# Order of the opening loads in a two-layer decoder trunk: the first weight tile goes to one queue, a second queue is held back behind an activation

## The chip, the cores and the metric

The kernel runs on one core of a Trainium2 chip. A core has five engines that run side by side, each with its own instruction stream: TensorE (PE, matrix products; its weight loads are a row of their own, PEld), VectorE (DVE), ScalarE (ACT), GpSimd (POOL) and SyncE (SP). Loads from the memory of the chip (DMA) are issued by an instruction of one of these streams; here SP and ScalarE issue the loads of the opening, and each has a queue of its own (SP's is q1 in the profile, ScalarE's is q10). A queue's name followed by q (SPq, ACTq) marks the issuing instruction in the profile.

The metric is device time in microseconds (us), the median of several runs.

## The reference

A decoder trunk of two layers on a sequence of 256 tokens and a model width of 1024, in float32. Every layer is an FFN, a token mixer and a second FFN, with norms around each; the mixer of layer 0 is a gated linear recurrence, that of layer 1 attention. Only the first FFN's beginning matters here:

```
def rms_norm(x, g):
    y = xf * lax.rsqrt(jnp.mean(xf * xf, axis=-1, keepdims=True) + EPS)
    return (y * g.astype(jnp.float32)).astype(x.dtype)

def swiglu(x, w_gate, w_up, w_down):
    return (jax.nn.silu(x @ w_gate) * (x @ w_up)) @ w_down
...
    for layer in range(DEPTH):
        f = swiglu(rms_norm(h, ffn1_pre_g[layer]), ffn1_w_gate[layer], ffn1_w_up[layer], ffn1_w_down[layer])
        h = h + 0.5 * rms_norm(f, ffn1_post_g[layer])
```

`ffn1_w_gate` has 1024 rows and 2816 columns per layer.

## The kernel before

The 256 tokens are two tiles of 128 rows, `h[0]` and `h[1]`, each 1024 columns wide (eight blocks of 128). A weight matrix is read in tiles of 128 x 1024 numbers (`raw`): for the first FFN that is two blocks of 128 rows by 512 columns side by side. Five `raw` buffers go round.

Products are made in a split form for precision: each operand is taken as an upper part, rounded to the product's format (`whi`, `xhi`), and a lower part, the rest (`wlo`, `xlo`). One product is then three: upper by upper, lower weight by upper x, and upper weight by lower x. The upper part of a weight tile is rounded by ScalarE (or by VectorE, where `dve=True`), the lower part is subtracted on VectorE.

x enters the products transposed. `turn(t, a, b, bank)` (L1136) transposes column blocks a to b of token tile t on TensorE; `x_up` (L1142, ScalarE) scales them by the norm's gains and rounds, `x_lo` (L1147, VectorE) makes the lower part. `w_up` and `w_lo` (L1123, L1130) do the same for half a weight tile or a whole one. `products(t, i, order)` (L1153) issues the products of token tile t with weight tile i in a given order: in a code such as `0uu`, `0lu`, `0ul`, the digit is the half of the weight tile, the first letter the weight's part and the second x's part.

The opening, L1101 to L1218, is written out by hand: the order of the lines is the order on each engine. It loads x (`load_h(t, a, b, queue)`, column blocks a to b of tile t) and the first four weight tiles (`load_w(i, a, b, queue)`, halves a to b of tile i), SP's queue being the default. Ahead of it, in program order, stand the load of the gains `grow0` (L113, ScalarE's queue), the set-up of an identity matrix on GpSimd and an activation of one column, `warm` (L119), ahead of which ScalarE loads the table of its functions. `keep_busy(n)` (L121) issues n products of constants that nobody reads. The rest of the program (L1219 on) is laid out by loops and a planner; SP's queue carries all of its weight loads.

Every load announces its end on one of eight semaphores, taken in turn. A load that takes a semaphore a second time waits first until the earlier load on it has landed. So in the opening the ninth load and those after it can wait for earlier ones; in the version before these are: `load_w(1, 1, 2)` on ScalarE's queue waits for `load_h(0, 0, 2)`, `load_w(2, 0, 2)` for the gains, `load_h(1, 4, 8)` for `load_w(0, 0, 1)`, and `load_w(3, 0, 2)` for `load_h(0, 2, 4)`.

The lines of the first products, before:

```
    keep_busy(6)
    gains_T(grow0, 16, 0)
    turn(0, 0, 1, gtbank())
    turn(0, 1, 2, gtbank())
    keep_busy(3)
    x_up(0, 0, 2)
    w_up(0, 0, 1, dve=True)
    x_lo(0, 0, 1)
    w_lo(0, 0, 1)
    w_up(0, 1, 2)
    x_lo(0, 1, 2)
    w_lo(0, 1, 2)
    products(0, 0, "0uu 0ul 1uu 0lu 1ul")
    turn(1, 0, 2, early[0])
```

Of the kernel before, what the change touches and what calls it, by code (L numbers as in the profile page):

```python
# [12 lines left out]
AF = mybir.ActivationFunctionType  # L13
# [31 lines left out]
def trunk_kernel(ctx: ExitStack, tc: tile.TileContext, A: dict, out: bass.AP):  # L45
    nc = tc.nc
# [18 lines left out]
    def gtbank():  # L65
        return psum.tile([P, 512], F32, tag="gt", name=nm("gt"), bufs=2)

    def trbank():
        return psum.tile([P, 512], F32, tag="tr", name=nm("tr"), bufs=2)
# [36 lines left out]
    h = [hpool.tile([P, D], F32, tag=f"h{t}", name=f"h{t}") for t in range(2)]  # L106

    def load_h(t, a, b, q=nc.sync):

        q.dma_start(h[t][:, a * P:b * P], A["x"][0, t * P:(t + 1) * P, a * P:b * P])  # L110
# [5 lines left out]
    mhalf = cpool.tile([P, 1], F32, name="mhalf")  # L116
    nc.gpsimd.memset(mhalf, -0.5)
    warm = cpool.tile([P, 1], F32, name="warm")
    nc.scalar.activation(warm, mhalf, AF.Silu)  # L119

    def keep_busy(n):  # L121

        ps = trbank()
        for _ in range(n):
            nc.tensor.matmul(ps, nc.const_aps.tensor(1.0, (P, P), BF16), nc.const_aps.tensor(1.0, (P, 512), BF16),
                             start=True, stop=True)
# [978 lines left out]
    def load_w(i, a, b, q=nc.sync):  # L1105

        q.dma_start(raws[i][:, a * 512:b * 512].rearrange("p (k n) -> p k n", k=b - a),
                          A["ffn1_w_gate"][0, (2 * i + a) * P:(2 * i + b) * P, :512].rearrange("(k p) n -> p k n", p=P))

    load_h(0, 0, 2)  # L1110
    load_w(0, 0, 1)
    load_w(0, 1, 2, nc.scalar)
    load_h(0, 2, 4)
    load_h(1, 0, 4, nc.scalar)
    load_w(1, 0, 1)
    load_w(1, 1, 2, nc.scalar)
    load_h(0, 4, 8)
# [18 lines left out]
    def turn(t, a, b, bank):  # L1136

        for k in range(a, b):
            tps[t, k] = bank[:, (k - a) * P:(k - a + 1) * P]
            nc.tensor.transpose(tps[t, k], h[t][:, k * P:(k + 1) * P], ident)  # L1140

    def x_up(t, a, b):  # L1142
        for k in range(a, b):
            nc.scalar.activation(xhi[:, k, t * P:(t + 1) * P], tps[t, k], AF.Copy,
                                 scale=gT[:, k:k + 1])
# [19 lines left out]
    gains_T(grow0, 16, 0)  # L1165
    turn(0, 0, 1, gtbank())
    turn(0, 1, 2, gtbank())
    keep_busy(3)
    x_up(0, 0, 2)
    w_up(0, 0, 1, dve=True)  # L1170
    x_lo(0, 0, 1)
# [139 lines left out]
```

## Time and profile before

| what | value |
|---|---|
| median of 3 runs | 1001.75 us |
| the runs | 1003.43, 1001.75, 1001.18 us |
| the profiled execution, its own time | 1001.1 us |
| its span, first to last instruction | 999.4 us |
| its mean granted TensorE clock | 0.998 |
| instructions | 12928 |
| moved by DMA | 178.88 MB, mean 179 GB/s |

The profile is one execution, recorded by the hardware. Its time, 1001.1 us, is 1.7 us more than its span. A row of the timeline reads: start, duration, engine, line of the kernel, operation, what is written, an arrow, what is read, the shapes, how many, and in brackets how long the engine had been idle before and what ended that. A row of the table of stretches reads: from and to, the sum of the window, then for PE, PEld, DVE, ACT and POOL the busy us and the number of instructions, the granted TensorE clock, the share in which the 16 DMA engines were busy, and GB/s. A row on a DMA queue reads: packets, MB, and the time that they took as a share of the 16 engines' time. Busy times of PE include a modelled end of each product, so the distance between two starts is the better measure of its pace.

### The profile page before, as it was taken

How to read it: one execution, taken by the hardware profiler on the slowest of the kernel's cores; microseconds unless marked ns; L12 is line 12 of the kernel's file. 1: busy time of each engine (PE TensorE's matmuls, PEld its weight loads, DVE VectorE, ACT ScalarE, POOL GpSimd, SP SyncE). 2: the span in 40 equal slices, each digit the busy share in tenths (PEclk: the TensorE clock that was granted, in tenths of full speed). 3: DMA queues.
4: the chain of work that ended last, by engine and by line, in shares of the span. 5: the costliest groups of instructions: out<-in, count | busy, mean ns of one | idle time of the engine just before them, and what ended most of it. 6: DMA issues, size and time to landing. Idle time of an engine off the chain costs nothing.

```text
span 999.4 us, 12928 instructions
## 1 busy us (share of the span) xinstructions
PE 991.0 (99%) x4792; PEld 829.4 (83%) x4792; DVE 613.0 (61%) x775; ACT 532.7 (53%) x749; POOL 59.0 (6%) x98
## 2 busy tenths in 40 slices
PE   9999999999999999999999999999999999999997
PEld 6888888899988888888898888888888888888885
DVE  6756554668998555554786655554487576555542
ACT  7545444569986544443564544443466565444431
POOL 2400000100004000000100000000033000000000
PEclk9999999999999999999999999999999999999999
DMA  8867556565336766555467666555455066665531
GB/s 289 308 191 208 183 186 192 158 189 157 119 115 217 216 175 196 182 186 190 130 208 233 172 188 188 189 179 191 157 173 167 15 200 210 190 187 190 190 106 42
DMA packets 92788, 178.88 MB, mean 179 GB/s; under 512 B 11982, under 2 KB 32886, under 8 KB 92726
## 3 DMA queue, kind: packets, MB, share of 16 engines
q1 hardware_dynamic: 91430, 177.16, 55.9%
q8 instruction: 37, 0.61, 0.2%
q10 hardware_dynamic: 464, 0.79, 0.2%
q0 software_dynamic: 832, 0.12, 0.1%
q14 instruction: 25, 0.20, 0.1%
HBM read 176.95 MB, written 1.05 MB: 178 GB/s over the span
## 4 chain that ended last, share of the span: by engine, by line
PE 99%; DMA 0%; DVE 0%; POOLq 0%; ACT 0%; issue 0%; DVEq 0%; SPq 0%; POOL 0%; ACTq 0%
PE mm L185 29%; PE mm L187 29%; PE mm L186 29%; PE tr L499 2%; PE gt L727 2%; PE mm L1159 1%; PE gt L1018 1%; PE mm L192 1%; PE mm L194 1%; PE mm L1045 1%; PE mm L193 1%; PE gt L216 1%; PE tr L1034 1%; DMA raw<-in_ffn_w_gate_dram 0%; PE tr L914 0%; PE tr L796 0%
## 5 line engine op out<-in xcount | busy, mean ns | idle before, releaser
L179 DVE TENSOR_TENSOR wlo<-raw,whi 128x1024 fp32r<-128x1024 f32 (+4 forms) x325 | 391.5, 1210 | 269.6 <-ACT whi L174 267.0
L174 ACT ACTIVATE whi<-raw 128x1024 fp32r<-128x1024 f32 (+4 forms) x325 | 337.8, 1045 | 315.7 <-PE mm L187 252.6
L185 PE MATMUL mm<-whi,xhi 128*128 128x512 f32 (+2 forms) x768 | 304.1, 396 | 0.0
L187 PE MATMUL mm<-whi,xlo 128*128 128x512 f32 (+2 forms) x768 | 298.8, 389 | 0.0
L186 PE MATMUL mm<-wlo,xhi 128*128 128x512 f32 (+2 forms) x768 | 298.1, 388 | 0.0
L187 PEld LDWEIGHTS mm<-whi,xlo 128*128 128x128 f32 x768 | 144.2, 188 | 30.3 <-DVE xlo L251 0.3
L186 PEld LDWEIGHTS mm<-wlo,xhi 128*128 128x128 f32 x768 | 144.5, 188 | 28.0 <-DVE wlo L179 0.3
L185 PEld LDWEIGHTS mm<-whi,xhi 128*128 128x128 f32 x768 | 144.3, 188 | 27.6
L185 PE MATMUL mm<-whi,hhi 128*128 128x512 f32 x352 | 138.6, 394 | 0.0
L187 PE MATMUL mm<-whi,hlo 128*128 128x512 f32 x352 | 137.9, 392 | 0.0
L186 PE MATMUL mm<-wlo,hhi 128*128 128x512 f32 x352 | 137.2, 390 | 0.0
L187 PEld LDWEIGHTS mm<-whi,hlo 128*128 128x128 f32 x352 | 66.1, 188 | 14.4
L186 PEld LDWEIGHTS mm<-wlo,hhi 128*128 128x128 f32 x352 | 66.1, 188 | 14.1
L185 PEld LDWEIGHTS mm<-whi,hhi 128*128 128x128 f32 x352 | 66.1, 188 | 13.5
L200 POOL TENSOR_SCALAR nv<-ss 128x1 f32<-128x1 f32 x24 | 11.6, 484 | 881.6 <-ACT junk L207 881.6
L493 DVE SCALAR_TENSOR_TENSOR prod<-mm,rstd,sil 128x512 f32<-128x512 f32 (+1 forms) x48 | 33.9, 705 | 38.0 <-PE mm L187 34.3
L484 ACT ACTIVATE sil<-mm,rstd 128x512 f32<-128x512 f32 (+1 forms) x48 | 31.2, 652 | 40.2 <-PE mm L187 40.2
L503 ACT ACTIVATE hhi<-tr 128x512 fp32r<-128x512 f32 (+1 forms) x48 | 26.6, 555 | 15.5 <-PE tr L499 15.4
L272 DVE TENSOR_TENSOR t<-mm,gb 128x512 f32<-128x512 f32 x24 | 16.2, 686 | 28.4 <-ACT junk L207 28.4
L504 DVE TENSOR_TENSOR hlo<-tr,hhi 128x512 fp32r<-128x512 f32 (+1 forms) x48 | 30.5, 642 | 1.4
L207 ACT ACTIVATE junk<-mm 128x512 bf16<-128x512 f32 x24 | 14.3, 596 | 31.7 <-PE mm L187 31.7
L185 PE MATMUL mm<-whi,zhi 128*128 128x340 f32 (+2 forms) x80 | 28.3, 354 | 0.0
(196 smaller groups left out, 934.0 us busy)
## 6 DMA issues: line engine op xcount, KB each, us to landing
raw<-in_ffn_w_down_dram SPq DMA_DIRECT2D x88, 512.0 KB
raw<-in_ffn_w_up_dram SPq DMA_DIRECT2D x80, 512.0 KB
raw<-in_ffn_w_gate_dram SPq DMA_DIRECT2D x78, 512.0 KB
raw<-in_rg_w_in_dram SPq DMA_DIRECT2D x20, 504.0 KB
raw<-in_rg_w_out_dram SPq DMA_DIRECT2D x10, 504.0 KB
raw<-in_ffn_w_gate_dram SPq DMA_DIRECT2D x18, 256.0 KB
raw<-in_ffn_w_up_dram SPq DMA_DIRECT2D x16, 256.0 KB
raw<-in_w_kv_dram SPq DMA_DIRECT2D x8, 512.0 KB
```

Source lines behind the costliest of these rows:

```text
L174: up = nc.scalar.activation(hi[:parts, c:c + m], rawv[:, c:c + m], AF.Copy)
L179: low.tensor_tensor(lo[:parts, c:c + m], rawv[:, c:c + m], hi[:parts, c:c + m].bitcast(F32), ALU.subtract)
L185: nc.tensor.matmul(ps, xh, wh, start=first, stop=False)
L186: nc.tensor.matmul(ps, xh, wl, start=False, stop=False)
L187: nc.tensor.matmul(ps, xl, wh, start=False, stop=last)
L272: nc.vector.tensor_tensor(t1[n], pf[n], gb[:, n * 512:(n + 1) * 512], ALU.mult)
L484: nc.scalar.activation(s[:, :nn], ps, AF.Silu, scale=rs[t][:, 0:1])
L493: nc.vector.scalar_tensor_tensor(pr[:, :nn], ps, rs[t][:, 0:1], s, ALU.mult, ALU.mult)
L499: nc.tensor.transpose(tp[:, j * P:(j + 1) * P], pr[:, j * P:(j + 1) * P], ident)
L503: nc.scalar.activation(hv, tp[:, :nn], AF.Copy)
L504: nc.vector.tensor_tensor(lv, tp[:, :nn], hv.bitcast(F32), ALU.subtract)
L727: nc.tensor.matmul(ps[:w, j * S:(j + 1) * S], wv[:, o:o + w], xc[:w, k, :], start=k == 0, stop=k == m - 1)
```

## The change

Three things are changed. The activation of one column on ScalarE writes column 0 of `h[1]`, and no longer the tile `warm` (which stays allocated). As `load_h(1, 0, 4)` writes the same column later, that load, on ScalarE's queue, now waits until the activation has run. The second half of the first weight tile, `load_w(0, 1, 2)`, moves from ScalarE's queue to SP's, behind the first half, and `load_h(1, 0, 4)` comes ahead of `load_h(0, 2, 4)` in program order (they are on different queues). The second `keep_busy` issues two products and not three.

```
     warm = cpool.tile([P, 1], F32, name="warm")
-    nc.scalar.activation(warm, mhalf, AF.Silu)
+
+    nc.scalar.activation(h[1][:, :1], mhalf, AF.Silu)
...
     load_h(0, 0, 2)
     load_w(0, 0, 1)
-    load_w(0, 1, 2, nc.scalar)
+    load_w(0, 1, 2)
+    load_h(1, 0, 4, nc.scalar)
     load_h(0, 2, 4)
-    load_h(1, 0, 4, nc.scalar)
     load_w(1, 0, 1)
     load_w(1, 1, 2, nc.scalar)
...
     turn(0, 1, 2, gtbank())
-    keep_busy(3)
+    keep_busy(2)
     x_up(0, 0, 2)
```

The order of loads on each queue, as built:

| queue | before | after |
|---|---|---|
| SP | `load_h(0,0,2)`, `load_w(0,0,1)`, `load_h(0,2,4)`, `load_w(1,0,1)`, `load_h(0,4,8)`, `load_w(2,0,2)`, `load_h(1,4,8)`, `load_w(3,0,2)` | `load_h(0,0,2)`, `load_w(0,0,1)`, `load_w(0,1,2)`, `load_h(0,2,4)`, `load_w(1,0,1)`, `load_h(0,4,8)`, `load_w(2,0,2)`, `load_h(1,4,8)`, `load_w(3,0,2)` |
| ScalarE | gains, `load_w(0,1,2)`, `load_h(1,0,4)`, `load_w(1,1,2)` | gains, (activation), `load_h(1,0,4)`, `load_w(1,1,2)` |

The waits for a semaphore taken again move with the order: now `load_h(0, 4, 8)` waits for the gains, `load_w(2, 0, 2)` for `load_h(0, 0, 2)`, `load_h(1, 4, 8)` for `load_w(0, 0, 1)`, and `load_w(3, 0, 2)` for `load_w(0, 1, 2)`; `load_w(1, 1, 2)` waits for none. Everything behind the opening stands in the same order on every engine.

More of the change, by code (lines that the diff above doesn't have):

```diff
@@ L118, in trunk_kernel @@
     warm = cpool.tile([P, 1], F32, name="warm")
-    nc.scalar.activation(warm, mhalf, AF.Silu)
+    nc.scalar.activation(h[1][:, :1], mhalf, AF.Silu)
     def keep_busy(n):
@@ L1111, in trunk_kernel @@
     load_w(0, 0, 1)
-    load_w(0, 1, 2, nc.scalar)
+    load_w(0, 1, 2)
+    load_h(1, 0, 4, nc.scalar)
     load_h(0, 2, 4)
-    load_h(1, 0, 4, nc.scalar)
     load_w(1, 0, 1)
@@ L1167, in trunk_kernel @@
     turn(0, 1, 2, gtbank())
-    keep_busy(3)
+    keep_busy(2)
     x_up(0, 0, 2)
```

## The prediction

> **What bounds the kernel now.** I read the page first: its busy shares and its chain of waits followed back from the end.
>
> ```profile
> span 999.4 us, 12928 instructions
> PE 991.0 (99%) x4792; PEld 829.4 (83%) x4792; DVE 613.0 (61%) x775; ACT 532.7 (53%) x749; POOL 59.0 (6%) x98
> PE 99%; DMA 0%; DVE 0%; POOLq 0%; ACT 0%; issue 0%; DVEq 0%; SPq 0%; POOL 0%; ACTq 0%
> ```
>
> TensorE is busy for 991.0 of 999.4 us and the chain that sets the end lies on it for 99%. An edit of the opening can therefore pay only what it takes off the time before TensorE works without a break. The built programs hold the same instructions in the same order on every engine behind the opening, so nothing else moves. Next I read the chain in order of time for the first 14 us.
>
> ```profile
> 1.23 4.38 DMA raw<-in_ffn_w_gate_dram
> ...
> 5.63 0.44 DVE whi L1126
> 6.07 0.14 issue
> 6.20 1.53 PE mm L1159 x5
> ```
>
> The end hangs on the landing of one load, the first half of the first weight tile (call it w0a; w0b is the other half, h0a the first two column blocks of x tile 0, h1a the first four of tile 1, w1a and w1b the halves of the second weight tile). It was issued at 1.23 and had landed 4.38 later, at 5.61; then come its rounding on VectorE, a hand-over of 0.14, and products. So 6.20 us is the figure that the edit can attack. Third, the timeline of that stretch: who issues when, and who waits for what.
>
> ```profile
> 0.80 0.38 SPq L110 DMA_DIRECT2D h<-in_x_dram  x1
> 1.31 0.37 ACTq L1107 DMA_DIRECT2D raw<-in_ffn_w_gate_dram  x1
> 1.71 0.45 ACTq L110 DMA_DIRECT2D h<-in_x_dram  x1
> 2.17 0.43 SPq L1107 DMA_DIRECT2D raw<-in_ffn_w_gate_dram  x1
> 2.53 0.20 ACT L119 ACTIVATE warm<-mhalf 128x1 f32<-128x1 f32 x1
> 2.64 0.43 SPq L110 DMA_DIRECT2D h<-in_x_dram  x1
> 3.12 0.43 SPq L1107 DMA_DIRECT2D raw<-in_ffn_w_gate_dram  x1
> 3.31 0.34 ACTq L1107 DMA_DIRECT2D raw<-in_ffn_w_gate_dram  x1
> 5.82 0.63 ACT L1128 ACTIVATE whi<-raw 128x512 fp32r<-128x512 f32 x1 [0.98 <-DMA raw<-in_ffn_w_gate_dram]
> 6.20 0.47 PE L1159 MATMUL mm<-whi,xhi 128*128 128x512 f32 x1 [0.57 <-DVE whi L1126]
> 6.51 0.39 PE L1159 MATMUL mm<-whi,xlo 128*128 128x512 f32 x1
> 6.74 0.40 PE L1159 MATMUL mm<-whi,xhi 128*128 128x512 f32 x1
> 6.83 0.34 DVE L1149 SCALAR_TENSOR_TENSOR xlo<-gt,gT,xhi 128x128 fp32r<-128x128 f32 x1
> 6.97 0.50 PE L1159 MATMUL mm<-wlo,xhi 128*128 128x512 f32 x1
> 7.32 0.41 PE L1159 MATMUL mm<-whi,xlo 128*128 128x512 f32 x1
> 7.57 0.38 PE L1140 MATMUL mm<-ident,h 128*128 128x128 f32 x2
> ```
>
> ScalarE began w0b's upper part at 5.82, after 0.98 us of waiting for the load: w0b landed only 0.2 behind w0a. Five products run from 6.20, then the transposes of h1a at 7.57. Two gaps exceed the pace of 0.23 (6.51 to 6.74): after 6.20, and 6.97 to 7.32, where the product waited for the `xlo` that VectorE ran from 6.83 to 7.17.
>
> **The loads, part by part.** w0b moves from ScalarE's queue (1.31) to SP's third place; a place in SP's queue is 0.47 (2.17, 2.64), so w0b is issued at 1.70, h0b at 2.17, w1a at 2.64. h1a now waits for the activation (2.53 + 0.20), so it is issued at about 2.8 and not 1.71; behind it on ScalarE's queue only w1b waits (issued about 3.25, before 3.31) and then the first `x_up`, which needs transposes at 3.7 and is not delayed. To see what this does to landings I use bytes: GB/s is KB per ms, so one row of the stretches of 1 us gives KB moved, and the queue rows tell whose.
>
> ```profile
> 1.00:2.00 1.00, 1.00 (x3) 0.30 (x2) 0.00 (x0) 0.76 (x1) 0.32 (x2) 1.00 0.08 25
> 2.00:3.00 1.00, 1.00 (x4) 0.30 (x2) 0.00 (x0) 0.72 (x2) 0.00 (x0) 1.00 0.92 205
> 3.00:4.00 1.00, 1.00 (x5) 0.48 (x4) 0.17 (x1) 0.00 (x0) 0.00 (x0) 1.00 0.89 266
> 4.00:5.00 1.00, 1.00 (x4) 0.42 (x3) 0.00 (x0) 0.62 (x2) 0.00 (x0) 1.00 0.99 329
> 5.00:6.00 1.00, 0.63 (x2) 0.00 (x0) 0.37 (x2) 0.18 (x1) 0.00 (x0) 1.00 1.05 378
> ```
>
> Together 25, 230, 496, 825 and 1203 KB had moved at 2, 3, 4, 5 and 6 us. The next fence has the queue rows, q1 being SP's and q10 ScalarE's: the first two for 0 to 4.5 us, then q10 in 6 to 7, 7 to 8 and 8 to 9.
>
> ```profile
> q1 hardware_dynamic: 305, 0.41, 35.0%
> q10 hardware_dynamic: 156, 0.24, 17.9%
> ...
> q10 hardware_dynamic: 8, 0.01, 5.0%
> ...
> q10 hardware_dynamic: 67, 0.14, 38.1%
> ...
> q10 hardware_dynamic: 71, 0.12, 32.2%
> ```
>
> By shapes h0a is 131 KB, each weight half and h1a 262, the gains row 8. SP's queue had moved h0a and w0a (0.39 MB) at about 4.45, yet w0a landed at 5.61: 1.15 us from nominal last byte to landing. ScalarE's queue had moved 0.27 MB at about 4.65 (0.24 at 4.5) and w0b landed near 5.80: 1.15 again. I use that lag throughout.
>
> *w0a.* With ScalarE's queue silent, 401 KB (gains, h0a, w0a) are through at 3 + (401 - 230)/266 = 3.64, landing at 4.8; at the slower 205 of the stretch before, 3.83 and 5.0. Earlier by 0.6 to 0.8. Rounding 0.44 and hand-over 0.14: the first product could start at 5.4.
>
> *w0b.* It now stands behind w0a in one queue. Nominal end at 663 KB: 4 + (663 - 496)/329 = 4.51, landing 5.66, if h1a stays out. h1a's first bytes are unknown: SP's first load took about 1.05 us from issue to bytes (0.80 to near 1.85, from 25 KB), ScalarE's first weight load about 1.7 (1.31 to near 3.0, as q10 had moved hardly anything by then). From 2.8 that is 3.85 to 4.5. At 4.5 it is too late to matter: 5.66. At 3.85, 456 KB are through, w0b lacks 207, and at half of 329 that takes 1.26: landing 6.26. I take the middle, 4.2: 562 KB through, 101 lacking, 0.61, nominal 4.81, landing 5.96. That is 0.16 *later* than before: w0b no longer has a queue to itself.
>
> [...]
>
> *The products.* ScalarE rounds w0b in 0.63: 5.98 to 6.61, so the third product, the first on w0b, starts at about 6.66 (before 6.74). The two ahead of it, at 5.4 and 5.6, are out of the way. VectorE's first four steps, rounding to the second `xlo`, took 5.63 to 7.17; from 4.82 they end at 6.36, so that `xlo` no longer holds the fifth product. So products at 6.66, 6.89, 7.12, transposes at 7.35 in place of 7.57: **0.22 us earlier**. By the bounds of w0b the third product starts at 6.36 or 6.96 and the transposes at 7.05 or 7.65: 0.52 earlier to 0.08 later.
>
> *h1a* must have landed by 7.35. From 4.2 at half of 329 to 378 (about 180) it needs 1.46, nominal 5.66, landing 6.8: covered, with 0.5 to spare. If first bytes come at 4.5 it lands at 7.1, which only the best case would feel, by 0.05.
>
> *The keep-busy matmul.* Its pace is the distance between the weight loads of the warm-up (rows of the timeline).
>
> ```profile
> 0.83 2.72 PE L125 MATMUL tr<-const-bfloat16-1.0 128*128 128x512 bf16 x6 [0.83 <-PEq L1296]
> 1.21 0.15 PEld L125 LDWEIGHTS <-const-bfloat16-1.0 128*128 128x128 bf16 x1 [0.28 <-issue]
> 1.64 0.15 PEld L125 LDWEIGHTS <-const-bfloat16-1.0 128*128 128x128 bf16 x1 [0.28 <-issue]
> 4.18 1.45 PE L125 MATMUL tr<-const-bfloat16-1.0 128*128 128x512 bf16 x3
> ```
>
> 0.43 each, three from 4.18, so TensorE is free at 5.46 before and at 5.04 after. A product at 5.4 would lose 0.06 to the third; as w0b decides at 6.66, the removal itself is worth 0 here.
>
> **What comes late next.** A gain at 7.35 survives only if the next loads don't hold TensorE.
>
> ```profile
> 9.62 0.63 ACT L1128 ACTIVATE whi<-raw 128x512 fp32r<-128x512 f32 x1 [0.34 <-DMA raw<-in_ffn_w_gate_dram]
> 10.13 0.40 PE L1159 MATMUL mm<-wlo,xhi 128*128 128x512 f32 x1
> 10.37 0.44 PE L1159 MATMUL mm<-whi,xhi 128*128 128x512 f32 x1
> ```
>
> w1b landed at about 9.6 and the product at 10.37 took it without slack (10.13 + 0.23). It was issued at 3.31, 0.2 behind SP's 3.12, yet q10 was idle from 6 to 7 and moved it in 7 to 9: it stood behind what SP had issued. After the change SP's load of 2.64 stands at 3.12 and that of 3.12 at about 3.6, so w1b goes ahead of the latter, straight behind h1a: from 5.66 at about 180, nominal 7.1, landing 8.3; other end unchanged, 9.6. I take it as out of the way.
>
> w1a has 1.32 MB up to and including it: at the last stretch's 378 that is 6 + (1320 - 1203)/378 = 6.31, landing 7.46. VectorE comes free for it when its fifth step ends, 6.61 + 0.68 = 7.3, so it may wait 0.2; TensorE then still has transposes and products of block pair 0 that do not need it.
>
> Sum: 1001.1 (profiled execution: span 999.4 and 1.7 around it) - 0.22 = 1000.9. The median of the runs, 1001.75, lies 0.65 above that execution, so I forecast 1001.5.
>
> **Rivals.** (a) *Swallowed at w1b*: it keeps its landing at 9.6, the product at 10.37 stays, gain 0: 1001.75. For it: no slack there. Against: its new place in the order. (b) *w0a does not land earlier*, because the 1.15 us lag and not sharing sets it: the first product stays at 6.20, the chain is the old one, 1001.75; the 0.6 us by which the bytes come sooner speak against it. (c) *The held-back load collides*: h1a enters at 3.85, w0b lands at 6.26, the transposes are at 7.65: 0.08 lost, 1001.85. (d) *TensorE stays slow*, the slower side. Warm-up matmuls and first products have the same 512 columns, but 0.43 against 0.23 apart: TensorE ran at half pace until somewhere between the third keep-busy (4.18 + 2 x 0.43 = 5.04) and 6.51. The profile's clock column does not show that (1.00 throughout). If the shorter warm-up and the new hole (two products at 5.4 and 5.6, then nothing until 6.66) start the count anew at 5.4, and it takes 4.2 to 5.7 us as it did from 0.83, products go at 0.43 until 9.6 to 11.1: from 6.66 that is 2.9 to 4.4 us, 7 to 10 products, 0.2 each: 1.4 to 2.0 lost less 0.22: 1002.9 to 1003.5. It decides once the hole exceeds what the hole of 5.46 to 6.20 already was (0.74); the new holes are 0.36 and about 0.83. [...]
>
> **How the numbers follow.** Forecast 0.45, (a) 0.17, (b) 0.10, (c) 0.10, (d) 0.15, 0.03 for a larger gain. 0.2% is 2 us, about what a measurement of this kernel can tell from no change; only the top of (d) together with a run like 1003.43 goes past 1003.75: slower 0.05. No case reaches 999.75: faster 0.04. Same 0.91. The likeliest case's own range is 1001.2 to 1001.85; the scatter of the runs and most of (d) widen it to 1000.5 to 1003.1.
>
> **What would show it.** Right: w0a's rounding starts near 4.8, w0b's near 6.0, the third product near 6.66, the transposes of h1a near 7.35 without a wait, w1b's rounding without an idle time before it, and every later product about 0.2 earlier. Wrong: first products 0.43 apart, an idle TensorE ahead of the transposes of h1a, w1b again at 9.6, or w0b's rounding later than 6.3.

## The result, and the profile after

| | before | changed |
|---|---|---|
| median of 16 runs | 1001.40 us | 1002.96 us |
| lowest, highest | 1000.75, 1003.43 | 1001.79, 1005.63 |
| the profiled execution (its span) | 1001.1 (999.4) | 1002.14 (1000.4) |

The changed kernel is slower by 1.6 us: ratio 1.0015, 95% interval 1.0008 to 1.0022. A small gain had been forecast. The first view of the profile after is the chain of waits in order of time, for the first 14 us (start, length, what; line numbers behind L119 are one higher than before).

```profile
2.53 0.21 ACT h L120
2.74 0.02 issue
2.77 5.64 DMA h<-in_x_dram
8.40 0.04 issue
8.45 0.44 PE mm L1141 x2
8.89 0.22 PE tr L1141 x2
```

The chain no longer runs through the first weight half. It runs through the activation, the load that waits for it, x tile 1, issued at 2.77 and landed at 8.40, and the transposes of that tile at 8.45. The timeline shows what stood in front of it.

```profile
2.77 0.36 ACTq L110 DMA_DIRECT2D h<-in_x_dram  x1
4.20 0.43 DVE L1127 CAST whi<-raw 128x512 fp32r<-128x512 f32 x1 [0.22 <-DMA raw<-in_ffn_w_gate_dram]
4.77 0.90 PE L1160 MATMUL mm<-whi,xhi 128*128 128x512 f32 x1
4.93 0.63 ACT L1129 ACTIVATE whi<-raw 128x512 fp32r<-128x512 f32 x1
5.89 0.58 PE L1160 MATMUL mm<-whi,xhi 128*128 128x512 f32 x1
6.30 0.39 PE L1160 MATMUL mm<-wlo,xhi 128*128 128x512 f32 x1
6.53 0.40 PE L1160 MATMUL mm<-whi,xlo 128*128 128x512 f32 x1
8.45 0.44 PE L1141 MATMUL mm<-ident,h 128*128 128x128 f32 x2 [1.52 <-DMA h<-in_x_dram]
10.66 0.63 ACT L1129 ACTIVATE whi<-raw 128x512 fp32r<-128x512 f32 x1 [0.44 <-DMA raw<-in_ffn_w_gate_dram]
```

The first weight tile came far earlier: its halves were being rounded at 4.20 and 4.93 (before 5.63 and 5.82), and the fifth product started at 6.53 (7.32). Then TensorE stood still until 8.45. The transposes, at 7.57 before, are 0.88 later; at the hand-over to the loop-built part, the first product of L185 before and of L186 after, it is 1.04:

```profile
19.26 0.40 PE L185 MATMUL mm<-whi,xhi 128*128 128x512 f32 x1
```

```profile
20.30 0.40 PE L186 MATMUL mm<-whi,xhi 128*128 128x512 f32 x1
```

From there on TensorE loses nothing more: the two spans, 999.4 and 1000.4, differ by 1.0 as well. In the table of stretches the 780 us from 200 to 980 are the same to 0.01 us of TensorE work, the first row from the profile before, the second from after:

```profile
200.00:980.00 780.00, 779.98 (x3846) 658.70 (x3846) 488.18 (x607) 423.70 (x596) 37.53 (x51) 1.00 0.55 173
```

```profile
200.00:980.00 780.00, 779.97 (x3846) 658.70 (x3845) 489.37 (x609) 424.69 (x598) 37.67 (x51) 1.00 0.55 173
```

So the profiled execution lost 1.04 us, all of it ahead of 20 us. The median lost 1.56. The rest shows in the granted clock that each of the 16 runs reports: in nine it is 0.998 or 0.999, their median 1002.24; in seven it is 0.996 or 0.997, their median 1004.18. The first group is 0.84 above before, about what the stall costs. The second has something on top, 1.9 us, that hardly ever met the version before: 2 of its 77 runs beside the experiments had such a clock. (The clock does not sort the runs without fault: one of the nine, with 0.998, took 1003.67.)

The stretches of 1 us of the changed kernel show where x tile 1 was in the meantime (last column GB/s, that is, KB per us).

```profile
1.00:2.00 1.00, 1.00 (x3) 0.30 (x2) 0.00 (x0) 0.76 (x1) 0.32 (x2) 1.00 0.07 23
2.00:3.00 1.00, 1.00 (x4) 0.30 (x2) 0.00 (x0) 0.72 (x2) 0.00 (x0) 1.00 0.86 197
3.00:4.00 1.00, 1.00 (x5) 0.48 (x4) 0.17 (x1) 0.00 (x0) 0.00 (x0) 1.00 1.04 393
4.00:5.00 1.00, 1.00 (x5) 0.53 (x3) 0.80 (x3) 0.69 (x3) 0.00 (x0) 1.00 0.66 175
5.00:6.00 1.00, 1.00 (x4) 0.75 (x4) 1.00 (x3) 0.56 (x1) 0.00 (x0) 1.00 0.65 153
6.00:7.00 1.00, 0.93 (x4) 0.41 (x2) 0.42 (x1) 0.00 (x0) 0.00 (x0) 1.00 0.98 307
```

SP's queue alone moved 393 KB in the stretch from 3 to 4. Then both together fell to 175 and 153, in the two stretches in which ScalarE's queue came in, and in 5 to 6 only 0.07 MB of it were ScalarE's (the first two rows below; q10 is ScalarE's, q1 SP's). In 6 to 7 they were 0.13 (the third row):

```profile
q1 hardware_dynamic: 60, 0.08, 35.2%
q10 hardware_dynamic: 36, 0.07, 29.9%
...
q10 hardware_dynamic: 70, 0.13, 42.5%
```

The same view for 4 to 5 gives ScalarE's queue 0.01 MB, all of it after 4.5. By 5.0 SP's queue had moved 0.77 MB; what it had issued up to 2.17 (`load_h(0, 0, 2)`, both halves of the first weight tile, `load_h(0, 2, 4)`) is 0.79.

### The profile page after: what moved, and what is told of

It is laid out like the page before. It is cut to its first block, busy times and chain, and to the rows that moved or that the text cites. A ratio compares the mean times of both kernels' runs of the same rounds, so it can differ in the third digit from the quotient of the medians.

```text
span 1000.4 us, 12926 instructions
## 1 busy us (share of the span) xinstructions
PE 991.1 (99%) x4791; PEld 829.8 (83%) x4791; DVE 613.4 (61%) x775; ACT 532.6 (53%) x749; POOL 59.2 (6%) x98
## 3 DMA queue, kind: packets, MB, share of 16 engines
HBM read 176.95 MB, written 1.05 MB: 178 GB/s over the span
## 4 chain that ended last, share of the span: by engine, by line
PE 98%; DMA 1%; ACT 0%; DVE 0%; POOLq 0%; ACTq 0%; issue 0%; DVEq 0%; POOL 0%
PE mm L186 29%; PE mm L188 29%; PE mm L187 29%; PE tr L500 2%; PE gt L728 2%; PE gt L1019 1%; PE mm L193 1%; PE mm L195 1%; PE mm L1046 1%; PE mm L194 1%; PE mm L1160 1%; PE gt L217 1%; DMA h<-in_x_dram 1%; PE tr L1035 1%; PE tr L915 0%; PE tr L797 0%
## 5 line engine op out<-in xcount | busy, mean ns | idle before, releaser
L186 PE MATMUL mm<-whi,xhi 128*128 128x512 f32 (+2 forms) x768 | 304.2, 396 | 0.0
L186 PEld LDWEIGHTS mm<-whi,xhi 128*128 128x128 f32 x768 | 144.3, 188 | 27.5
L186 PE MATMUL mm<-whi,hhi 128*128 128x512 f32 x352 | 138.6, 394 | 0.0
L186 PEld LDWEIGHTS mm<-whi,hhi 128*128 128x128 f32 x352 | 66.1, 188 | 13.5
L186 PE MATMUL mm<-whi,zhi 128*128 128x340 f32 (+2 forms) x80 | 28.3, 354 | 0.0
```

The lines of the kernel that those rows point to most:

```text
L186: nc.tensor.matmul(ps, xh, wh, start=first, stop=False)
```

## The experiments

All times are medians; each ratio is against runs of the version before on the same chip (1001.42, 1001.47 and 1001.37 us in the three groups of runs). "Low clock" counts runs whose granted clock was 0.997 or less. An edit is shown against the changed kernel, unless another version is named. Every landing and every start is read from one trace, so differences of a few tenths between two kernels say little. Three theories were open at first: H, the held-back x tile 1 comes too late; Q (later S), starting a second queue beside a busy one slows both; G, the missing warm-up matmul.

**The missing warm-up matmul alone**, against the version before

```
-    keep_busy(3)
+    keep_busy(2)
```

> The version before with one keep-busy matmul less, its only edit. Theory H (the held-back load of x tile 1 comes too late and TensorE waits for it) and rival Q (ScalarE's queue, when it starts beside SP's, slows both for about 1.5 us) expect no change: ratio within 0.9997 to 1.0003, first product at 6.20. Rival G (the shorter warm-up keeps TensorE at half pace for longer) expects a good part of the whole difference of 1.5 us here: 1.0005 to 1.0015, with products 0.43 apart behind 6.20.

Measured: 1001.67 us, ratio 1.0003 (0.9994 to 1.0011). By this interval alone up to 1.1 us could still be here, so it does not settle G. The changed kernel's trace does for its execution: the fifth product stands 0.23 behind the fourth (6.30, 6.53) and TensorE then waits 1.52 us for a load, so a slow start cost it nothing; and none of the four one-queue versions below, with two matmuls as well, is slower than before. The profiled execution here, 1002.55 and the highest of its 11, shows what G meant. The first products were still 0.42 to 0.43 apart, where before they came down to 0.23:

```profile
6.54 0.63 PE L1159 MATMUL mm<-whi,xlo 128*128 128x512 f32 x1
6.97 0.63 PE L1159 MATMUL mm<-whi,xhi 128*128 128x512 f32 x1
7.39 0.63 PE L1159 MATMUL mm<-wlo,xhi 128*128 128x512 f32 x1
```

The full pace came only behind 9.81, and the transposes stood at 8.25 in place of 7.57. The granted clock of this stretch reads 1.00 all the same: the slow pace of the start is seen in the distances and not in that column. Whether it is more frequent with two matmuls is not shown; 4 of 11 runs lay above 1002 us here, and 7 of the 29 of before.

**The change without the hold**

```
-    nc.scalar.activation(h[1][:, :1], mhalf, AF.Silu)
+    nc.scalar.activation(warm, mhalf, AF.Silu)
```

> The change without the hold: the activation writes its own tile, so ScalarE's queue issues the load of x tile 1 at about 1.3 and not 2.8. H: that load lands before 6.8, TensorE does not wait for it, and the time is 0.3 to 0.9 us below the version before (0.9991 to 0.9997). Q: the slow stretch comes at about 3.0 to 4.5 in place of 4.5 to 6.0, the first weight half lands near 5 again and the time is that of before (0.9997 to 1.0003). G: still 0.5 to 1.5 us above before.

Measured: 1002.97 us, 1.0014 (1.0005 to 1.0023), low clock in 6 of 11. H and Q had the time wrong. G had it about right (0.5 to 1.5 us above before), but not the way: the first two products below are 0.31 apart, not 0.43. x tile 1 did come early (TensorE did not wait for it), and now the *second weight half* was late: it stands behind the first in SP's queue, and ScalarE began to round it at 6.91, after 2.07 us of waiting for the load (at 4.93 in the change). On ScalarE's queue x tile 1 and the second half of the second weight tile, which is needed later, had been issued at 1.31 and 1.71.

```profile
6.11 0.47 PE L1160 MATMUL mm<-whi,xhi 128*128 128x512 f32 x1 [1.02 <-DVE whi L1127]
6.42 0.40 PE L1160 MATMUL mm<-whi,xlo 128*128 128x512 f32 x1
7.59 0.50 PE L1160 MATMUL mm<-whi,xhi 128*128 128x512 f32 x1 [0.77 <-ACT whi L1129]
...
8.50 0.63 PE L1141 MATMUL mm<-ident,h 128*128 128x128 f32 x2
```

The third product waited until 7.59 and the transposes came at 8.50, as late as in the change. In the stretches of the same trace DMA moved 381 and 388 in 4 to 6; the slow stretch came in 3 to 4, with 211, at the time that Q had named. The stretches behind 8 show something else, the granted clock (the column ahead of the DMA share):

```profile
8.00:9.00 1.00, 1.00 (x6) 0.77 (x5) 0.60 (x2) 0.00 (x0) 0.00 (x0) 0.62 1.05 391
9.00:10.00 1.00, 1.00 (x6) 0.82 (x5) 0.17 (x1) 0.63 (x2) 0.00 (x0) 0.50 1.05 401
10.00:11.00 1.00, 1.00 (x4) 0.87 (x4) 1.00 (x3) 0.55 (x3) 0.00 (x0) 0.50 1.06 401
11.00:12.00 1.00, 1.00 (x4) 0.79 (x3) 0.93 (x4) 1.00 (x5) 0.00 (x0) 0.68 1.05 393
```

After the holes ahead of 6.11 and 7.59, waits of 1.02 and 0.77 us, TensorE ran at half clock: with the clock at either 1.00 or the 0.50 of the two middle rows, an estimate, it lasted twice what is missing from 1.00 in the four rows, 0.76 + 1 + 1 + 0.64 = 3.4 us. Products were 0.43 apart in it (11.06 and 11.49) and 0.23 behind it (12.27 and 12.50). What sets its length, and how long a wait brings it on, this trace does not show.

**The hold without the move of the weight half**: the version before with only

```
-    nc.scalar.activation(warm, mhalf, AF.Silu)
+    nc.scalar.activation(h[1][:, :1], mhalf, AF.Silu)
```

> The version before with the hold alone: the second weight half stays on ScalarE's queue at 1.31, the load of x tile 1 behind it waits for the activation (2.8). H: that load lands about 1 us later than before and TensorE waits ahead of its transposes: 0.3 to 1 us slower (1.0003 to 1.0010). Q: ScalarE's queue starts near 3.0 as before, the load stands behind the weight half in it anyway, so no change (0.9998 to 1.0003).

Measured: 1003.23 us, 1.0027 (1.0015 to 1.0040), low clock in 3 of 7: the slowest of all. The fifth product is at 6.87, the transposes only at

```profile
9.30 0.44 PE L1140 MATMUL mm<-ident,h 128*128 128x128 f32 x2 [2.00 <-DMA h<-in_x_dram]
```

H had the sign and the place, and about half of the size (1.8 us by the medians; the ratio stands higher, as three of seven runs took 1005 or more). So the hold alone is enough for a loss of this size, and the move without the hold was enough too: in each case one load that TensorE needs next came late.

**All opening loads on SP's queue, nothing held** (the gains stay on ScalarE's):

```
-    nc.scalar.activation(h[1][:, :1], mhalf, AF.Silu)
+    nc.scalar.activation(warm, mhalf, AF.Silu)
...
-    load_h(1, 0, 4, nc.scalar)
+    load_h(1, 0, 4)
...
-    load_w(1, 1, 2, nc.scalar)
+    load_w(1, 1, 2)
```

> All opening loads but the gains on SP's queue, x tile 1 right behind the first weight tile, nothing held, two keep-busy matmuls. H and Q: with ScalarE's queue silent SP's goes on at about 390 KB per us, x tile 1 has landed by 5.5 to 6, the products start at 4.8 and the transposes follow without a wait: 0.5 to 1.2 us below before (0.9988 to 0.9995). If the slow stretch behind 4.5 us has nothing to do with the second queue (the memory or the making of descriptors), it comes here too, x tile 1 lands near 8 and the time is above before.

Measured: 1000.48 us, 0.9990 (0.9981 to 0.9998), from 999.98 to 1000.61, low clock in none of 11. This version beats both kernels, and its runs lie closer together than any other's. H and Q both expected that, so it does not choose between them; G's loss is not here, though it has the two warm-up matmuls as well. x tile 1 was later than forecast (5.5 to 6): TensorE waited 0.34 for it.

```profile
4.68 0.74 PE L1160 MATMUL mm<-whi,xhi 128*128 128x512 f32 x1
...
6.12 0.40 PE L1160 MATMUL mm<-whi,xlo 128*128 128x512 f32 x1
6.86 0.44 PE L1141 MATMUL mm<-ident,h 128*128 128x128 f32 x2 [0.34 <-DMA h<-in_x_dram]
```

**Late issue, or another queue?** The same, but with the hold, so that x tile 1 is issued as late as in the change, only on SP's queue:

```
-    load_h(1, 0, 4, nc.scalar)
+    load_h(1, 0, 4)
...
-    load_w(1, 1, 2, nc.scalar)
+    load_w(1, 1, 2)
```

> The changed kernel with the two loads of ScalarE's queue (x tile 1 and the second half of the second weight tile) at the same places of SP's queue; the hold stays, so SP issues x tile 1 at about 2.8, the same time as the change does on ScalarE's queue. Theory S (what is lost comes from starting a second queue beside a busy one, not from the late issue): x tile 1 lands by 7.5, TensorE waits at most 0.8, time below the version before: 0.9990 to 0.9998. Rival L (the late issue is what costs): it lands near 8.4 as in the change and the time is 1.0008 to 1.0020.

Measured: 1000.92 us, 0.9993 (0.9984 to 1.0002), low clock in none of 11.

```profile
2.76 0.80 SPq L110 DMA_DIRECT2D h<-in_x_dram  x2
...
6.33 0.44 PE L1141 MATMUL mm<-ident,h 128*128 128x128 f32 x2
```

Issued at 2.76, as in the change at 2.77, x tile 1 was there for transposes at 6.33 without a wait, not 8.45. The issue time by itself is not the cause; L falls. But S is not shown by it either, though its numbers came true: DMA slowed here too, on one queue, from 397 KB per us in 3 to 4 to the 226 of the stretch from 4 to 6 (last column), and the edit also changes the order.

```profile
4.00:6.00 2.00, 1.82 (x8) 0.94 (x7) 1.82 (x5) 1.26 (x3) 0.00 (x0) 1.00 0.82 226
```

On SP's queue x tile 1 is issued ahead of all that SP issues later: the hold keeps back `load_h(0, 2, 4)` (here right behind it, the second of the two from 2.76, and at 2.17 in the change) and the second weight tile (3.60, in the change 2.65) too.

**The same place in the order, one queue**: x tile 1 behind the first half of the second weight tile, nothing held (SP's order: `load_w(1, 0, 1)`, `load_h(1, 0, 4)`, `load_w(1, 1, 2)`; the changed kernel's lines otherwise).

```
-    nc.scalar.activation(h[1][:, :1], mhalf, AF.Silu)
+    nc.scalar.activation(warm, mhalf, AF.Silu)
...
-    load_h(1, 0, 4, nc.scalar)
     load_h(0, 2, 4)
     load_w(1, 0, 1)
-    load_w(1, 1, 2, nc.scalar)
+    load_h(1, 0, 4)
+    load_w(1, 1, 2)
```

> All opening loads on SP's queue without the hold, but x tile 1 behind the first half of the second weight tile, which is the order of bytes that the change has by its issue times. S: by then 1.3 MB have to pass at about 320 KB per us, x tile 1 lands at 7 to 7.6, TensorE waits 0.5 to 1.2, ratio 0.9993 to 1.0000. Rival B (the order of bytes explains the loss, the second queue does not): x tile 1 lands near 8.4, ratio 1.0008 to 1.0020.

Measured: 1001.42 us, 1.0000 (0.9991 to 1.0008), low clock in none of 11.

```profile
7.83 0.44 PE L1141 MATMUL mm<-ident,h 128*128 128x128 f32 x2 [1.12 <-DMA h<-in_x_dram]
```

The wait of 1.12 and the ratio are what S expected; x tile 1 landed about 0.2 later than its 7.6. B falls: the order of bytes alone did not make this kernel slower than before. The later place has its price all the same, 0.97 us of the transposes' start and 0.94 of the median against the one-queue version above. What the change loses beyond it, 1.5 us of the median, came only with loads on ScalarE's queue.

**x tile 1 alone on the second queue**, held; the weight half behind it goes to SP:

```
-    load_w(1, 1, 2, nc.scalar)
+    load_w(1, 1, 2)
```

> The changed kernel with only x tile 1 left on ScalarE's queue (held); the second half of the second weight tile goes to SP's queue. S: the start of ScalarE's queue near 4.5 still slows both, x tile 1 lands near 8, TensorE waits over 1 us, ratio 1.0003 to 1.0015. Rival W (the weight half behind x tile 1 on the second queue takes the bandwidth): x tile 1 lands before 7.3 and the ratio is under 1.0000.

Measured: 1001.99 us, 1.0007 (0.9998 to 1.0016), low clock in 4 of 11: those four lie at 1003.3 to 1003.6, the other seven at 1001.5 to 1002.4.

```profile
8.18 0.44 PE L1141 MATMUL mm<-ident,h 128*128 128x128 f32 x2 [1.54 <-DMA h<-in_x_dram]
```

W falls: x tile 1 landed near 8.2 and not before 7.3, and the weight half behind it costs 0.27 (8.45 - 8.18), no more than single traces can differ by. S has its numbers here too (near 8, over 1 us of waiting, 1.0003 to 1.0015), but the interval takes in 1.0000.

**The hole filled**: six keep-busy matmuls put where TensorE stood still.

```
     products(0, 0, "0uu 0ul 1uu 0lu 1ul")
+    keep_busy(6)
     turn(1, 0, 2, early[0])
```

> The changed kernel with six more keep-busy matmuls between the fifth product and the transposes of x tile 1, where TensorE stood still. They take about 1.3 us at full pace and 2.6 at half pace, against a hole of 1.5 to 2. Theory G2 (in many runs the hole also makes TensorE fall back to half pace, which is the spread of 1001.8 to 1005.6): median down to 1002.0 to 1002.5, highest run under 1003.5. Rival (the hole is all there is): median stays at 1002.7 to 1003.2 with the same spread, or rises.

Measured: 1002.24 us, 1.0009 (1.0000 to 1.0018), highest 1003.32, low clock in none of 11. The transposes were at 8.76 in its trace, behind 0.81 of idle time that the six matmuls left, so x tile 1 was as late, yet the seven-in-sixteen share of low clocks is gone, and the median is the 1002.24 that the changed kernel has in its full-clock runs. G2 holds.

**The changed kernel twice more**

> The changed kernel once more, for a second trace. If its loss is one of order, x tile 1 lands between 8 and 9 again and TensorE waits over 1.2 us ahead of its transposes. If the landing of 8.4 was chance, it lands before 7.5. If the clock gate closes behind the hole, the stretches of 1 us show a granted clock of 0.50 for about 3.4 us after 8.

> The changed kernel a third time, with the same expectations as the second.

Measured: 1004.61 us (clock 0.997) and 1002.17 us (0.998), one run each. Transposes at 9.66 after 2.78 of waiting in the first (later than the 8 to 9 expected), at 8.60 after 2.09 in the second; the late landing is no chance. In the first the granted clock fell to 0.50 behind the hole, which is what the expectation calls the closing of the clock gate. The stretches:

```profile
7.00:8.00 1.00, 0.00 (x0) 0.00 (x0) 0.00 (x0) 0.00 (x0) 0.00 (x0) 1.00 1.02 330
8.00:9.00 1.00, 0.00 (x0) 0.00 (x0) 0.00 (x0) 0.00 (x0) 0.00 (x0) 1.00 0.97 342
9.00:10.00 1.00, 0.34 (x2) 0.34 (x3) 0.43 (x1) 0.00 (x0) 0.00 (x0) 0.75 1.02 389
10.00:11.00 1.00, 1.00 (x5) 0.82 (x4) 0.00 (x0) 0.61 (x2) 0.00 (x0) 0.50 1.05 408
11.00:12.00 1.00, 1.00 (x5) 0.90 (x4) 0.95 (x3) 0.34 (x3) 0.00 (x0) 0.50 1.05 361
12.00:13.00 1.00, 1.00 (x4) 0.81 (x3) 0.93 (x4) 1.00 (x5) 0.00 (x0) 0.54 1.03 387
```

TensorE did nothing for two whole stretches, and half clock follows, reckoned as above, for 0.5 + 1 + 1 + 0.9 = 3.4 us. Products were 0.42 and 0.43 apart in it (11.86, 12.28, 12.71), and 0.23 in the second trace, whose clock stayed at 1.00 (10.06, 10.29). At half clock 3.4 us hold the work of an estimated 1.7 at full clock: 1.7 us lost, against the 1.9 between the two groups of the changed kernel's runs.

**x tile 1 in two halves, one queue**, against the one-queue version with nothing held

```
-    load_h(1, 0, 4)
+    load_h(1, 0, 2)
+    load_h(1, 2, 4)
```

> The one-queue kernel with x tile 1 loaded in two halves, so that the first transposes need 131 KB and not 262. If the landing of x tile 1 is what still holds the opening there (0.34 us of idle ahead of its transposes), the first half lands 0.4 to 0.8 earlier, the wait goes and the time falls to 1000.1 to 1000.4 where before runs 1001.4 (0.9986 to 0.9990). If the price of a further load (0.47 of issue, one more semaphore taken twice) eats it: 1000.4 to 1000.8.

Measured: 1000.79 us, 0.9992 (0.9983 to 1.0001). The wait ahead of the transposes went (they start at 6.61), but behind the further load the second weight tile was issued at 3.60 (3.12 without the split), VectorE did not begin to round it before 8.0 (7.84), and TensorE waited 0.23 at 8.87 for `xlo`, which stands behind that tile's rounding on VectorE. Nothing gained over the plain one-queue version.

## Why the prediction was wrong

- **Right: what bounds the kernel and how far the change reaches.** The loss lies ahead of 20 us, and the rest is unchanged.
- **Better than forecast: the first weight tile.** w0a's rounding was put at 4.8 and w0b's at 5.98; they began at 4.20 and 4.93. Two terms were mis-sized, the rate of SP's queue alone and the lag of 1.15 us from nominal last byte to landing. By the rows after, 401 KB are through at 3 + (401 - 220)/393 = 3.46 and not 3.64, and w0a had landed by 4.20: a lag of 0.74 or less. The third product came at 5.89 in place of 6.66.
- **The step that failed: "covered, with 0.5 to spare".** x tile 1 was to land at 6.8, from first bytes at 4.2, a half share of about 180 KB per us and the lag of 1.15. It landed at 8.40, and the transposes, put at 7.35, came at 8.45 behind the idle TensorE that the prediction names as a sign of being wrong. The lag held this time: with 0.01, 0.07 and 0.13 MB in the three stretches from 4 to 7, ScalarE's queue reached the tile's 0.26 near 7.3, 1.1 ahead of the landing. The other two terms failed. First bytes came between 4.5 and 5.0, no earlier than the late bound of 4.5, and the share was 70 and then 130 KB per us. The prediction took its rates from the profile before, in which DMA was busy without a break from 4 us on (a share of 0.95 to 1.05 in the four stretches up to 8); in the changed kernel both queues together moved 175 and 153 in 4 to 6. The edit had freed the first weight tile and made the next load that TensorE needs a late one: held to 2.77, with five loads of SP's issued ahead of it, on a queue that moved 0.07 of the 0.15 MB in 5 to 6. Its bytes began after 4.5, with 0.77 MB of SP's moved by 5.0. That fits a load that waits for what was issued ahead of it, but no run separates this from a delay of about 2 us of that queue.
- **Rival (c)**, the collision, had the right load but looked at its effect on w0b; the damage was to the load itself. Priced at 0.08 lost, it cost 0.88 in the profiled execution.
- **Rival (d)**, TensorE at half pace, had the slow pace and the wrong hole. Its price of 1.4 to 2.0 us is near the 1.7 and 1.9 found, but in the changed kernel's profile the half pace did not outlast the first five products: the second to the fourth were 0.43 and 0.41 apart, the fifth 0.23 behind the fourth. In the first of the two further traces full pace had come too (6.25 and 6.48); there the clock fell to 0.50 behind the wait for x tile 1. No run shows a count that starts anew behind a hole, as (d) supposed; how long a hole it takes is not settled. Counted from the fifth product's start to the transposes in the one trace of each kernel, low clocks came in none of 11 runs behind 7.83 - 6.31 = 1.52, 4 of 11 behind 8.18 - 6.25 = 1.93, 7 of 16 behind 8.45 - 6.53 = 1.92, 3 of 7 behind 9.30 - 6.87 = 2.43, and none of 11 where the hole was filled. But the hole differs from run to run of one kernel: 9.66 - 6.48 = 3.18 with half clock behind it and 8.60 - 6.11 = 2.49 without, in the two further traces. And without the hold half clock came behind two waits of 1.02 and 0.77 close together in the one trace, and low clocks in 6 of 11 runs.
- **Rivals (a) and (b)** did not come up: w0a did land earlier, and w1b, put at 8.3 to 9.6 and rounded at 10.66, was late behind a chain that was late already. It added about 0.1: the products around it were 0.93 late ahead of it (10.83, before 9.90) and 1.04 behind it (11.68, before 10.64).
- **The keep-busy matmul** was put at 0; its measurement, 1.0003 (0.9994 to 1.0011), neither confirms nor refutes that.
- **The start of the sum.** The forecast stood on a median of three runs, 1001.75; sixteen gave 1001.40, so the gain of 0.22 meant about 1001.2. And GB/s is KB per us, where the prediction has KB per ms; its sums go by the right unit.

The measured 1002.96 lies inside the stated range, and on the side where only 0.25 of the chance had been put, on (c) and (d) together. That it lies inside is luck: the range reaches so far because of the scatter and of (d), which looked at another hole, and no term held a wait for x tile 1.

What stays open is the slow stretch of DMA. In 5 to 6 it moved 153 to 249 KB per us in the change (three traces), with the hole filled, with x tile 1 alone on ScalarE's queue and in the two one-queue versions with x tile 1 later; it kept 332 in the plain one-queue version and 388 where both queues started early. Those two had a slow stretch too, at another time: 272 in 4 to 5 and 234 in 7 to 8 in the one, 211 in 3 to 4 in the other. Neither a second queue nor the order of loads separates those cases. So it is shown that x tile 1 came late (landed at 8.40), that this cost the stall (1.52 us of waiting) and, in part of the runs, the clock (7 of 16), and that an early place on SP's queue takes the loss away (1000.48 us); how its lateness divides between its place in the order and the second queue is not.

## What to carry to other kernels

Here a load was brought forward and another came late: the second half of the first weight tile was rounded 0.89 us earlier (4.93, before 5.82), and TensorE waited 1.52 us for x tile 1, issued behind it. Write down, for each load that TensorE needs next, what is issued ahead of it on every queue, and check the first one after those that were helped. The loads did best in the order of their need on one queue (1000.48 us, before 1001.42); with the same hold the transposes of x tile 1 started at 8.45 on the second queue and at 6.33 on one. Where a trace had TensorE wait 1.5 to 2.8 us for x tile 1, or 1.02 and 0.77 close together, low clocks came in 4 of 11 to 6 of 11 runs, and in the changed kernel the runs with them lay 1.9 us above the others: look at the granted clock of each run, and fill the hole (none of 11) or shorten it.

## What the runs showed of the hardware

Neither was expected. One queue alone reached 393 KB per us between 3 and 4 us, more than two queues did in the same stretch (266), so in that stretch two queues moved no more than one. And the versions with all opening loads but the gains on SP's queue repeat far better: from the lowest to the highest of 11 runs it is 0.63 to 0.86 us in the four of them, one with a wait of 1.12, against 1.76 to 4.27 (7 to 16 runs) in the six other versions and 1.64 to 2.68 (15 to 33 runs) in the groups of the version before. Why is not shown; the slow pace of the start, which the granted clock does not tell, may be part of it.
